# Turned attention rows in a scores bank, one norm per unit, and a memory head prepared ahead

## The chip, the core and the metric

The kernel runs on one core of a Trainium2 chip. The core's engines run side by side, each through its own list of instructions in order: TensorE (PE; its weight loads are PEld), VectorE (DVE), ScalarE (ACT), GpSimd (POOL) and SyncE (SP), which here only starts DMAs. PE writes into PSUM, eight banks of 2 KB a partition; only DVE and ACT read them in this kernel. The metric is the device time of one launch in microseconds (us). About 0.2% (6 us) is what a measurement of this kernel can tell from no change.

## What is computed

One sequence of 512 positions, 1024 channels, passes a hybrid layer and then two further layers, all in float32. Cut to what matters here:

```
x = x + 0.5 * swiglu(norm(x))                     # ffn f1, likewise f2, f3, f4
h = norm(x) @ w_in                                # q, keys and values, gates, conv, memory queries
nsa:  for each of 16 heads: compressed branch + selected branch + window branch,
      each softmax(q.k/8 + rel_bias, masked) @ v, weighted by gates
      (8 blocks of 64 with top 16: all blocks are selected, so both long branches are causal attention)
mem:  4 heads of 256: softmax(qm.km/16) @ vm over 256 memory rows
x = x + (g_nsa*nsa + g_conv*conv + g_mem*mem) @ w_out
second block: stick-breaking attention, ffn, gate; forgetting attention (16 heads, causal), ffn, gate
```

## The kernel before

Every float32 product is made of three matmuls: each operand is split into a rounded high part and a rest (`split`: ACT writes the high part, DVE subtracts), and `mm3` adds high.high, high.low and low.high. A dense step is one `mm3`, three matmuls of 512 columns; a job of eight steps is one 1024x128 weight tile. Its weights come by DMA as `raw` and are split into `wh` (ACT) and `wl` (DVE), three buffers of each.

PSUM is four tags of two banks: `d` for dense results, `s` for scores, `t` for transposes, `o` for attention output. A tag's two banks are used in turn: the third use of a tag waits until the first's readers are done.

`nsa` (from line 934) has 32 units, (head, branch) pairs. In step u of its loop (lines 1046 to 1085) PE makes the scores of unit u (`unit_scores`: three uses of `s`, two dense steps before the last), DVE adds the bias and takes the row minimum (L632), ACT takes the exponential and its row sum (L634), DVE inverts the sum (`RECIPROCAL`) and multiplies it by the gate, POOL scales the four row tiles `pr` (L910). Then the rows of unit u-1 are turned (`unit_turn`): ten 128x128 transposes in three groups, of four, four and two, each group in a bank of `t`, split into `pth` (ACT) and `ptl` (DVE). The third group therefore comes to the first group's bank. `nsa_out` multiplies the turned rows with the values (eight matmuls into `o`). `feed` and `pace` put dense steps of other work (convolution, gates, values) between these; `pinned` keeps PE's matmuls in the order written. DVE, ACT and POOL, and PE where nothing is pinned, are ordered by a scheduler.

`forget` (from line 1301) runs 16 units in the same way; its dense steps are the projections of the later heads and half of the output projection. `head_stats` and `head_norm` normalise queries and keys through banks of `o` and `s`; `normed` in nsa does one head pair, `norm` in forget two, one `s` bank each.

`memory` (from line 683) does four heads one after the other: norm and split of queries, keys and values, scores, softmax, transposes, a gate's dense job and the product. `transpose_rows` (from line 614) turns a row vector such as `rB` into a column `rT`, with one bank of `t` and one copy for each of its four transposes.

Of the kernel before, what the change touches and what calls it, by code (L numbers as in the profile page):

```python
# [12 lines left out]
AF = mybir.ActivationFunctionType  # L13
ALU = mybir.AluOpType
# [149 lines left out]
class Net:  # L164
# [449 lines left out]
    def transpose_rows(self, dst, src, n=S):  # L614

        nc = self.nc
        for i in range(n // P):
            ps = self.bank("t")
            nc.tensor.transpose(ps[:, :P], src[:, i * P : (i + 1) * P], self.ident)
            nc.vector.tensor_copy(dst[:, i : i + 1], ps[:, :1])  # L620


    def softmax_rows(self, pool, src, n, bias, st, i, tag, bufs):
# [59 lines left out]
    def memory(self):  # L683

        nc, tc = self.nc, self.tc
        with self.pool("mem", "left") as pool:
            self.tags = self.TAGS
            qm = []
            for n in range(KC):
                ps = self.dbank()  # L690
                self.dense(ps, self.a["w_qm"][n], self.h)
                q = self.t(pool, S, "qm", 8)
                nc.vector.tensor_tensor(q, ps, self.rB, op=ALU.mult)
                qm.append(q)
            qst = self.head_stats(qm, self.sel256, 2)
            self.tags = ("d",)
            for m in range(4):
                qr, kr = [], []
                for n in (2 * m, 2 * m + 1):
                    self.head_norm(qm[n], n, 2, qst, self.col("mqg")[:, n % 2 : n % 2 + 1])  # L700
                    hl = self.pair(pool, f"qr{n % 2}")
                    self.split(hl[0], hl[1], qm[n], -1.0 / 16.0)
                    qr.append(hl)
                    k = self.t(pool, NM, "kmr", 2)
                    nc.sync.dma_start(k, self.kmd[n * P : (n + 1) * P, :])
                    hl = self.pair(pool, f"kr{n % 2}", NM)
                    self.split(hl[0], hl[1], k)
                    kr.append(hl)
                vr = self.t(pool, S, "vmr", 2)
                nc.sync.dma_start(vr.rearrange("p (i c) -> p i c", i=2),  # L710
                                  self.vmd[:, :, m * 256 : m * 256 + 256].rearrange("i p c -> p i c"))
                vm = self.pair(pool, "vm", S)
                self.split(vm[0], vm[1], vr)
                st = self.t(pool, 2 * NT, "mst", 2)
# [8 lines left out]
                pt = []  # L723
                for i in range(NT):
                    nc.vector.tensor_scalar(pr[i], pr[i], st[:, i : i + 1], None, op0=ALU.mult)
                for b in range(2):
                    tp = self.bank("t")
                    for i in range(NT):
                        nc.tensor.transpose(tp[:, i * P : (i + 1) * P], pr[i][:, b * P : (b + 1) * P], self.ident)
                    hl = self.pair(pool, f"mt{b}")  # L730
                    self.split(hl[0], hl[1], tp)
                    pt.append(hl)
                for n in (2 * m, 2 * m + 1):
                    g = self.t(pool, S, "mg", 2)
                    pg = self.dbank()
                    self.dense(pg, self.a["w_mg"][2, n], self.h)
                    nc.vector.tensor_tensor(g, pg, self.rB, op=ALU.mult)
                    nc.scalar.activation(g, g, AF.Tanh, scale=0.5)
                    po = self.bank("o")
# [172 lines left out]
    def unit_turn(self, pool, pr):  # L912

        ph, pl = self.pair(pool, "pt", 1280, 1)
        for tiles, c0, n in (((0,), 0, 512), ((1, 3), 512, 512), ((2,), 1024, 256)):
            tp = self.bank("t")
            self.feed(2 * (tiles == (2,)))
            for j in tiles:
                for i in range(j, NT):
                    d = self.PT0[j] - c0 + (i - j) * P  # L920
# [13 lines left out]
    def nsa(self):  # L934
        nc, tc = self.nc, self.tc
        self.hv = 1
        with self.pool("nsa", "right") as pool:
# [108 lines left out]
            for u in range(33):  # L1046
# [3 lines left out]
                if u < 32:  # L1050
# [4 lines left out]
                    if br == 1 and u < 31:  # L1055
                        n = u + 1
                        tb = self.nsa_bias(pool, 4 * (2 * (n // 16) + n // 2 % 2) + n // 4 % 4)
                if u == 14:
                    next(cmp0)
                if rows:  # L1060
                    pt = self.unit_turn(pool, rows[0])
                    self.pace(upto - 2)
                    self.nsa_out(pool, V, pc, pt, *rows[1:])
                rows = (pr, a, r, b, br)
                if u == 9:
                    qst = self.head_stats(raw[1], self.sel64, 1, tag="o", fill=1)
                elif u == 10:
                    normed(1, 0, qst)
                    normed(1, 1, qst)
                elif u in (11, 12):  # L1070
                    normed(1, u - 9, qst)
                elif u == 13:
                    cmp0 = self.nsa_cmp(pool, 1, 0, [qn[1, k] for k in range(4)], kc, G, pc)
                    next(cmp0)
                elif u == 14:
# [3 lines left out]
                    kn[0] = keys(1, 0)  # L1079
                elif u == 15:  # L1080
                    next(cmp1)
                    kn[1] = keys(1, 1)
                elif u == 16:
                    next(cmp1, None)
                self.pace(upto)
            self.feed(999)
            self.pinned = False

# [212 lines left out]
    def forget(self):  # L1301
# [3 lines left out]
        with self.pool("fox", "left") as pool:  # L1305
# [73 lines left out]
            for u in range(17):  # L1379
                t, b = u // 2, u % 2  # L1380
                upto = base + (176 - base) * (u + 1) / 10 if u < 10 else 176 + 46 * (u - 9) / 7
                if u < 16:
# [2 lines left out]
                    self.unit_scale(pr, st)  # L1385
                    if u < 15:
                        fb = self.forget_bias(pool, u + 1)
                if rows:
                    pt = self.unit_turn(pool, rows[0])
                    self.pace(upto - 4)  # L1390
                    self.forget_out(pool, m + later, V, pt, *rows[1:])
                rows = (pr, t, b)
                if u % 4 == 1 and u < 13:
                    self.pace(48 * (u // 4 + 1) + 32)
                    hst = self.head_stats(xs[u // 4 + 1], self.sel64, 1, pool=pool, tag="o", fill=2)
                elif u % 4 in (2, 3) and u < 12:
                    n = 2 * (u // 4) + u % 4
                    kq[n] = norm(n, hst)
                self.pace(upto)
            self.feed(999)  # L1400
            self.pinned = False
            self.tags = self.TAGS
# [66 lines left out]
```

## Time and profile before

| what | us |
|---|---|
| median of 3 runs (2928.08 to 2933.24) | 2930.53 |
| the profiled execution | 2931.12 |
| its span, first to last instruction | 2929.3 |
| PE busy | 2858.3 (98%) |
| DVE busy | 1615.2 (55%) |
| ACT busy | 1212.9 (41%) |
| POOL busy | 238.7 (8%) |

The execution was 1.8 us longer than its span. A matmul counts as busy until its pipelined end, so the table's 98% hides short gaps; the views of waits and windows show them. The stages in the trace: memory about 438 to 565 us, the start of nsa to 714, its loop to 1066, the loop of forget 2275 to 2492. The rest is dense layers and the stick-breaking attention, which the change does not touch.

### The profile page before, as it was taken

To read this page: it belongs to the slowest core of one execution; us is meant where nothing else is said; L and a number is where in the kernel's file an instruction comes from. 1 tells how busy PE (TensorE), PEld (TensorE's weight loads), DVE (VectorE), ACT (ScalarE), POOL (GpSimd) and SP (SyncE) were. 2 spreads that over 40 slices of the span, in tenths; PEclk is the share of its full clock that TensorE was granted. 3 is DMA by queue.
4 is the path that set the end of the run, shared out by engine and by line. 5 is a ranking of instruction groups with operands and counts; after the bars stand their busy time and mean duration, and the time that the engine had idled before them with its cause. 6 is when DMAs were issued, how large, how long until landed. Compare 5 with 4: busy or idle time off the path is not lost.

```text
span 2929.3 us, 37143 instructions
## 1 busy us (share of the span) xinstructions
PE 2858.3 (98%) x13873; PEld 2367.6 (81%) x13874; DVE 1615.2 (55%) x2718; ACT 1212.9 (41%) x2078; POOL 238.7 (8%) x361
## 2 busy tenths in 40 slices
PE   9999999999989999999999999999999999999999
PEld 8888887778767888888888887888888777888887
DVE  7443345767666665443347877434357767544344
ACT  6322234344555544322235655223234555422223
POOL 0000000001223320000000000000003431000000
PEclk9999999999999999999999999999999999999999
DMA  7423342235233245323343335232333535522332
GB/s 240 111 94 101 103 131 90 90 119 148 74 98 93 90 142 180 101 94 99 106 130 109 97 104 199 94 101 92 99 99 130 155 101 154 182 100 94 96 93 99
DMA packets 133229, 339.19 MB, mean 116 GB/s; under 512 B 17415, under 2 KB 30215, under 8 KB 133048
## 3 DMA queue, kind: packets, MB, share of 16 engines
q1 hardware_dynamic: 132376, 335.49, 37.0%
q10 hardware_dynamic: 672, 1.32, 0.4%
q8 instruction: 109, 1.79, 0.2%
q14 instruction: 72, 0.59, 0.1%
HBM read 279.82 MB, written 28.61 MB: 105 GB/s over the span
## 4 chain that ended last, share of the span: by engine, by line
PE 63%; DVE 4%; issue 2%; DMA 1%; ACT 1%; POOL 0%; SPq 0%; DVEq 0%; ACTq 0%; POOLq 0%
PE d L190 22%; PE s L190 13%; PE o L190 13%; PE t L190 11%; PE t L195 1%; DMA qk<-xd 1%; DVE wl L219 1%; DVE pr L632 1%; DVE ptl L219 1%; DMA xd<-qk 1%; PE s L1288 0%; PE t L1288 0%; PE o L1298 0%; POOL mo L1172 0%; PE o L1299 0%
## 5 line engine op out<-in xcount | busy, mean ns | idle before, releaser
L209 ACT ACTIVATE wh<-raw 128x1024 fp32r<-128x1024 f32 (+3 forms) x499 | 493.5, 989 | 1205.9 <-PE d L190 339.9
L219 DVE TENSOR_TENSOR wl<-raw,wh 128x1024 fp32r<-128x1024 f32 (+3 forms) x499 | 576.7, 1156 | 302.7 <-ACT wh L209 299.8
L634 ACT ACTIVATE pr<-pr,st 128x128 f32<-128x128 f32 x192 | 106.1, 553 | 68.8 <-DVE st L632 67.9
L910 POOL TENSOR_SCALAR pr<-pr,st 128x128 f32<-128x128 f32 x192 | 106.2, 572 | 244.5 <-DVE st L1384 72.2
L195 PE MATMUL t<-idn,pr 128*128 128x128 f32 x480 | 70.5, 277 | 24.5 <-DVE ptl L219 21.7
L219 DVE TENSOR_TENSOR ptl<-t,pth 128x512 fp32r<-128x512 f32 x144 | 83.3, 595 | 19.4 <-ACT pth L209 18.5
L231 POOL TENSOR_TENSOR raw<-raw,cols 128x1024 f32<-128x1024 f32 x25 | 49.0, 1960 | 523.9 <-DMA xd<-x 466.9
L195 PEld LDWEIGHTS t<-idn,pr 128*128 128x128 f32 x480 | 54.9, 141 | 43.0 <-DVE ptl L219 33.6
L209 ACT ACTIVATE pth<-t 128x512 fp32r<-128x512 f32 x144 | 72.5, 521 | 36.0 <-PE t L195 34.8
L632 DVE CUSTOM_DVE_ANT_0 pr<-s,tb 128x128 f32<-128x128 f32 (+3 forms) x128 | 57.8, 486 | 33.9 <-PE s L190 15.8
L190 PE MATMUL o<-ptl,V 128*128 128x512 f32 x192 | 61.5, 331 | 3.3 <-DVE ptl L219 2.0
L483 ACT ACTIVATE on<-o 64x512 f32<-64x512 f32 x48 | 28.6, 595 | 74.8 <-PE o L190 60.4
L484 DVE TENSOR_TENSOR on<-o,on 64x512 f32<-64x512 f32 x48 | 32.7, 681 | 46.7 <-ACT on L483 46.5
L408 POOL MEMSET hrh<- 128x512 f32 (+2 forms) x10 | 4.7, 471 | 639.2 <-PE s L190 567.1
L190 PE MATMUL o<-pth,V 128*128 128x512 f32 x192 | 56.7, 321 | 0.0
L518 ACT ACTIVATE ta<-ta 128x512 f32<-128x512 f32 x88 | 55.3, 629 | 3.0 <-DVE ta L517 3.0
L190 PE MATMUL d<-h3h,wh 128*128 128x512 f32 x136 | 55.8, 411 | 0.0
L190 PE MATMUL d<-h2h,wh 128*128 128x512 f32 x136 | 55.8, 410 | 0.0
L190 PE MATMUL d<-h0h,wh 128*128 128x512 f32 x136 | 55.1, 405 | 0.4 <-DVE q2s L794 0.4
L190 PE MATMUL d<-h4h,wh 128*128 128x512 f32 x136 | 55.3, 407 | 0.0
L190 PE MATMUL d<-h0h,wl 128*128 128x512 f32 x136 | 53.5, 393 | 1.7 <-DVE wl L219 1.7
L519 DVE TENSOR_TENSOR ta<-s,ta 128x512 f32<-128x512 f32 x22 | 15.2, 692 | 71.2 <-PE s L190 71.2
(2175 smaller groups left out, 8652.8 us busy)
## 6 DMA issues: line engine op xcount, KB each, us to landing
raw<-in_f_in_dram SPq DMA_DIRECT2D x176, 512.0 KB
raw<-in_f_out_dram SPq DMA_DIRECT2D x64, 512.0 KB
raw<-in_f_out_dram SPq DMA_DIRECT2D x32, 384.0 KB
raw<-in_w_mg_dram SPq DMA_DIRECT2D x24, 512.0 KB
raw<-in_w_cv_dram SPq DMA_DIRECT2D x24, 512.0 KB
xd<-x SPq DMA_DIRECT2D x32, 256.0 KB
x<-xd SPq DMA_DIRECT2D x32, 256.0 KB
raw<-in_w_pg_dram SPq DMA_DIRECT2D x16, 512.0 KB
```

The source lines that it names most:

```text
L190: i = self.nc.tensor.matmul(out, lhs, rhs, **kw)
L195: i = self.nc.tensor.transpose(out, src, self.ident)
L209: nc.scalar.activation(h, src, AF.Copy, scale=1.0 if scale is None else scale)
L219: eng.tensor_tensor(lo, src, hb, op=ALU.subtract)
L231: nc.gpsimd.tensor_tensor(v, v, gain.unsqueeze(2).to_broadcast([P, gain.shape[1], n]), op=ALU.mult)
L483: self.nc.scalar.activation(dst[h], po[64:], AF.Copy)
L484: self.nc.vector.tensor_tensor(dst[h], po[:64], dst[h], op=ALU.add)
L518: nc.scalar.activation(ta, ta, AF.Silu)
L519: nc.vector.tensor_tensor(ta, pb, ta, op=ALU.mult)
L632: nc.vector.tensor_tensor_reduce(out=p, in0=src, in1=bias, op0=ALU.add, op1=ALU.min, scale=1.0, scalar=3e38, accum_out=m)
L634: nc.scalar.activation(p, p, AF.Exp, bias=m, scale=-1.0, accum_out=stat)
L910: self.nc.gpsimd.tensor_scalar(pr[i], pr[i], st[:, i : i + 1], 1.0, op0=ALU.mult, op1=ALU.mult)
```

## The change

The third group of a unit's turn goes to a bank of `s`, and no dense steps stand inside the turn. Three steps stand before it and one behind it; the rest of the unit's steps, at least two, come before the product, which is now the last thing in the unit. In nsa `normed` does one head a step (four steps, 10 to 13, where it was two in the first), and the compressed branch of the second half follows a step later. In memory the next head's operands and gates are issued between the softmax scaling and the transposes of the present one. `transpose_rows` writes its four transposes into one bank and copies once.

```diff
     def transpose_rows(self, dst, src, n=S):
+        ps = self.bank("t")
         for i in range(n // P):
-            ps = self.bank("t")
-            nc.tensor.transpose(ps[:, :P], src[:, i * P : (i + 1) * P], self.ident)
-            nc.vector.tensor_copy(dst[:, i : i + 1], ps[:, :1])
+            self.tr(ps[:, i * P : (i + 1) * P], src[:, i * P : (i + 1) * P])
+        nc.vector.tensor_copy(dst, ps.rearrange("p (i c) -> p i c", c=P)[:, : n // P, 0])
...  memory
+            def gates(m):     # the two dense jobs w_mg[2, n] of head m with their tanh, "mg" now 4 buffers
+            def operands(m):  # norm, split and loads of head m as before, "vm" now 2 buffers
+            gs = gates(0)
+            nxt = operands(0)
             for m in range(4):
+                qr, kr, vm = nxt
...
                     nc.vector.tensor_scalar(pr[i], pr[i], st[:, i : i + 1], None, op0=ALU.mult)
+                now = gs
+                if m < 3:
+                    nxt = operands(m + 1)
+                    gs = gates(m + 1)
...  unit_turn
         for tiles, c0, n in (((0,), 0, 512), ((1, 3), 512, 512), ((2,), 1024, 256)):
-            tp = self.bank("t")
-            self.feed(2 * (tiles == (2,)))
+            tp = self.bank("s" if tiles == (2,) else "t")
...  nsa, the loop over u
-                if u == 14:
-                    next(cmp0)
+                self.feed(3)
                 if rows:
                     pt = self.unit_turn(pool, rows[0])
-                    self.pace(upto - 2)
-                    self.nsa_out(pool, V, pc, pt, *rows[1:])
-                rows = (pr, a, r, b, br)
+                    self.feed(1)
...
-                elif u == 10:
-                    normed(1, 0, qst)
-                    normed(1, 1, qst)
-                elif u in (11, 12):
-                    normed(1, u - 9, qst)
-                elif u == 13:
+                elif 10 <= u <= 13:
+                    normed(1, u - 10, qst)
+                elif u == 14:
                     cmp0 = self.nsa_cmp(pool, 1, 0, [qn[1, k] for k in range(4)], kc, G, pc)
...
-                self.pace(upto)
+                self.pace(max(upto, self.steps + 2))
+                if rows:
+                    self.nsa_out(pool, V, pc, pt, *rows[1:])
+                rows = (pr, a, r, b, br)
...  forget, the loop over u
+                self.feed(4)
                 if rows:
                     pt = self.unit_turn(pool, rows[0])
-                    self.pace(upto - 4)
-                    self.forget_out(pool, m + later, V, pt, *rows[1:])
-                rows = (pr, t, b)
+                    self.feed(1)
...  head_stats and norm as before
-                self.pace(upto)
+                self.pace(max(upto, self.steps + 2))
+                if rows:
+                    self.forget_out(pool, m + later, V, pt, *rows[1:])
+                rows = (pr, t, b)
```

How the order moves, at three places. A row is an instruction of that engine, line, operation, what it writes and reads; `x2` merges equal ones.

PE in the loop of nsa, turn of the first unit, from the end of the second group, before:

```order
L195 MATMUL t_5966<-idn_148,pr_1088_5858 128x128 x2
L190 MATMUL d_5980<-h0h_77,wh_5773 128x512
L190 MATMUL d_5980<-h0l_78,wh_5773 128x512
L190 MATMUL d_5980<-h0h_77,wl_5774 128x512
L190 MATMUL d_5980<-h1h_79,wh_5773 128x512
L190 MATMUL d_5980<-h1l_80,wh_5773 128x512
L190 MATMUL d_5980<-h1h_79,wl_5774 128x512
L195 MATMUL t_5973<-idn_148,pr_1086_5838 128x128
L195 MATMUL t_5973<-idn_148,pr_1088_5858 128x128
L190 MATMUL d_5980<-h2h_81,wh_5773 128x512
```

and now:

```order
L195 MATMUL t_5974<-idn_148,pr_1084_5850 128x128 x2
L195 MATMUL s_5981<-idn_148,pr_1082_5830 128x128
L195 MATMUL s_5981<-idn_148,pr_1084_5850 128x128
L190 MATMUL d_5955<-h3h_83,wh_5765 128x512
L190 MATMUL d_5955<-h3l_84,wh_5765 128x512
L190 MATMUL d_5955<-h3h_83,wl_5766 128x512
L190 MATMUL d_5955<-h4h_85,wh_5765 128x512
L190 MATMUL d_5955<-h4l_86,wh_5765 128x512
L190 MATMUL d_5955<-h4h_85,wl_5766 128x512
L190 MATMUL d_5955<-h5h_87,wh_5765 128x512
L190 MATMUL d_5955<-h5l_88,wh_5765 128x512
```

The two transposes of the third group wrote `t_5973` behind six dense matmuls; they now write `s_5981` right behind the second group, and nine dense matmuls follow. Nine more now stand ahead of the turn.

DVE in a late unit of nsa, from the last score tile, before (`pr,st<-s,tb` is the softmax step of L632, `ptl<-t` the split of a turned group, `st<-st,G` the gate):

```order
L632 ISA pr_1728_9107,st_9080<-s_9104,tb_9014 128x512
L632 ISA st_9080 128x1
L219 TENSOR_TENSOR ptl_9117<-t_9118,pth_9116 128x512
L1052 RECIPROCAL st_9080<-st_9080 128x4
L1053 TENSOR_TENSOR st_9080<-st_9080,G_4487 128x4
L219 TENSOR_TENSOR ptl_9117<-t_9125,pth_9116 128x512
L219 TENSOR_TENSOR ptl_9117<-t_9132,pth_9116 128x256
L484 TENSOR_TENSOR on_9157<-o_9053,on_9157 64x512
```

and now:

```order
L632 ISA pr_1724_9105,st_9078<-s_9102,tb_9012 128x512
L632 ISA st_9078 128x1
L1068 RECIPROCAL st_9078<-st_9078 128x4
L1069 TENSOR_TENSOR st_9078<-st_9078,G_4479 128x4
L775 TENSOR_TENSOR cv_9027<-d_9057,cv_9027 128x512
L219 TENSOR_TENSOR wl_9334<-raw_9331,wh_9333 128x1024
L219 TENSOR_TENSOR ptl_9130<-t_9131,pth_9129 128x512
L779 SCALAR_TENSOR_TENSOR cv_9124<-cv_9027,cols_71,cv_9124 128x511
L219 TENSOR_TENSOR ptl_9130<-t_9138,pth_9129 128x512
L780 SCALAR_TENSOR_TENSOR cv_9124<-cv_9027,cols_71,cv_9124 128x510
L219 TENSOR_TENSOR ptl_9130<-s_9145,pth_9129 128x256
```

The three splits stood around the reciprocal; now the reciprocal and the gate, the convolution's multiplications (`cv`) and a weight split (`wl`) stand ahead of the splits and among them.

PE in forget, the norm of the next heads (`s<-hrh` and `s<-hrl`: two matmuls into one bank), before, behind the product:

```order
L190 MATMUL o_19402<-ptl_19370,V_18773 128x256
L190 MATMUL o_19402<-pth_19369,V_18773 128x256
L190 MATMUL s_19415<-hrh_19313,selr_151 128x512
L190 MATMUL s_19415<-hrl_19314,selr_151 128x512
L190 MATMUL s_19419<-hrh_19313,selr_151 128x512
L190 MATMUL s_19419<-hrl_19314,selr_151 128x512
L190 MATMUL d_19348<-wh_19092,h6h_89 128x256
```

and now, behind the turn:

```order
L195 MATMUL s_19402<-idn_148,pr_3484_19107 128x128
L195 MATMUL s_19402<-idn_148,pr_3486_19120 128x128
L190 MATMUL d_19376<-h3h_83,wh_19141 128x512
L190 MATMUL d_19376<-h3l_84,wh_19141 128x512
L190 MATMUL d_19376<-h3h_83,wl_19142 128x512
L190 MATMUL s_19410<-hrh_19281,selr_151 128x512
L190 MATMUL s_19410<-hrl_19282,selr_151 128x512
L190 MATMUL s_19414<-hrh_19281,selr_151 128x512
L190 MATMUL s_19414<-hrl_19282,selr_151 128x512
L190 MATMUL d_19376<-h4h_85,wh_19141 128x512
```

The norm moved from behind the product to three matmuls behind the third group. `s_19402` (third group), `s_19410` and `s_19414` are three uses of the tag `s` in a row.

## Rows read from the trace of the kernel before

**Rows 1.** The page, part 4: the chain that ended last, shares of the span

```profile
PE 63%; DVE 4%; issue 2%; DMA 1%; ACT 1%; POOL 0%; SPq 0%; DVEq 0%; ACTq 0%; POOLq 0%
```

**Rows 2.** Windows: length, busy us of PE, PEld, DVE, ACT, POOL; clock, DMA

```profile
438.00:565.00 127.00, 122.68 (x584) 97.16 (x583) 76.34 (x131) 57.73 (x105) 6.25 (x14) 1.00 0.28 94
...
714.00:1066.00 352.00, 326.26 (x1726) 271.58 (x1725) 224.86 (x551) 185.66 (x438) 100.58 (x150) 0.99 0.31 88
2283.00:2492.00 209.00, 198.82 (x1161) 163.22 (x1161) 152.03 (x324) 123.03 (x279) 62.81 (x80) 0.99 0.46 133
843.00:846.50 3.50, 3.50 (x10) 2.87 (x11) 0.92 (x2) 0.38 (x1) 1.52 (x3) 0.55 0.67 127
```

**Rows 3.** PE waits, 714:1066 (first loop): who for whom: us, times, longest

```profile
PE t L195 <- DVE ptl L219: 17.7, 18, 3.5
PE s L190 <- DVE st L632: 2.9, 3, 1.0
PE t L195 <- DVE st L1053: 2.5, 1, 2.5
PE o L190 <- DVE nrr L219: 1.9, 1, 1.9
```

**Rows 4.** PE timeline, one unit: start, us, what [idle before <-releaser]

```profile
744.72 1.03 PE L195 MATMUL t<-idn,pr 128*128 128x128 f32 x8
...
748.52 0.44 PE L195 MATMUL t<-idn,pr 128*128 128x128 f32 x2 [1.37 <-DVE ptl L219]
748.72 0.48 PE L190 MATMUL d<-h2h,wh 128*128 128x512 f32 x1
749.03 0.40 PE L190 MATMUL d<-h2l,wh 128*128 128x512 f32 x1
```

**Rows 5.** DVE timeline, the same unit

```profile
744.53 0.69 DVE L758 TENSOR_TENSOR cv<-d,cv 128x512 f32<-128x512 f32 x1 [0.58 <-PE d L190]
745.14 0.68 DVE L632 CUSTOM_DVE_ANT_0 pr<-s,tb 128x512 f32<-128x512 f32 x1
...
745.75 1.22 DVE L219 TENSOR_TENSOR wl<-raw,wh 128x1024 fp32r<-128x1024 f32 x1
746.88 0.75 DVE L762 SCALAR_TENSOR_TENSOR cv<-cv,cols,cv 128x511 f32<-128x511 f32 x1
...
747.77 0.69 DVE L219 TENSOR_TENSOR ptl<-t,pth 128x512 fp32r<-128x512 f32 x1
...
749.11 1.02 DVE L219 TENSOR_TENSOR ptl<-t,pth 128x512 fp32r<-128x512 f32 x2
```

**Rows 6.** ACT timeline, the same unit

```profile
744.67 1.04 ACT L209 ACTIVATE wh<-raw 128x1024 fp32r<-128x1024 f32 x1
...
746.32 0.71 ACT L634 ACTIVATE pr<-pr,st 128x512 f32<-128x512 f32 x1
```

**Rows 7.** DVE and then POOL timeline, a later unit

```profile
1001.01 2.28 DVE L219 TENSOR_TENSOR wl<-raw,wh 128x1024 fp32r<-128x1024 f32 x1 [0.18 <-ACT wh L209]
...
1000.91 1.29 POOL L754 TENSOR_TENSOR cv<-cv,rB 128x512 f32<-128x512 f32 x1 [1.44 <-DVE cv L753]
```

**Rows 8.** PE waits, 2275:2492 (second loop)

```profile
PE t L195 <- DVE ptl L219: 4.1, 5, 2.1
PE o L190 <- DVE ptl L219: 2.0, 4, 0.6
PE s L190 <- DVE x L423: 1.7, 4, 0.6
```

**Rows 9.** PE timeline, the four transposes of rB at the start of nsa

```profile
587.76 0.69 PE L619 MATMUL t<-idn,rB 128*128 128x128 f32 x2 [4.12 <-DVE rT L620]
...
589.10 0.63 PE L190 MATMUL d<-h2h,wh 128*128 128x512 f32 x1
589.52 0.63 PE L190 MATMUL d<-h2l,wh 128*128 128x512 f32 x1
```

**Rows 10.** PE waits, 438:565 (memory)

```profile
PE s L190 <- ACT mp L630: 2.9, 3, 1.5
```

More of the change, by code (lines that the diff above doesn't have):

```diff
@@ L696, in memory @@
             self.tags = ("d",)
-            for m in range(4):
+            def gates(m):
+                gs = []
+                for n in (2 * m, 2 * m + 1):
+                    g = self.t(pool, S, "mg", 4)
+                    pg = self.dbank()
+                    self.dense(pg, self.a["w_mg"][2, n], self.h)
+                    nc.vector.tensor_tensor(g, pg, self.rB, op=ALU.mult)
+                    nc.scalar.activation(g, g, AF.Tanh, scale=0.5)
+                    gs.append(g)
+                return gs
+            def operands(m):
                 qr, kr = [], []
@@ L711, in memory @@
                                   self.vmd[:, :, m * 256 : m * 256 + 256].rearrange("i p c -> p i c"))
-                vm = self.pair(pool, "vm", S)
+                vm = self.pair(pool, "vm", S, 2)
                 self.split(vm[0], vm[1], vr)
+                return qr, kr, vm
+            gs = gates(0)
+            nxt = operands(0)
+            for m in range(4):
+                qr, kr, vm = nxt
                 st = self.t(pool, 2 * NT, "mst", 2)
@@ L722, in memory @@
                 nc.vector.reciprocal(st[:, :NT], st[:, :NT])
-                pt = []
                 for i in range(NT):
                     nc.vector.tensor_scalar(pr[i], pr[i], st[:, i : i + 1], None, op0=ALU.mult)
+                now = gs
+                if m < 3:
+                    nxt = operands(m + 1)
+                    gs = gates(m + 1)
+                pt = []
                 for b in range(2):
@@ L728, in memory @@
                     for i in range(NT):
-                        nc.tensor.transpose(tp[:, i * P : (i + 1) * P], pr[i][:, b * P : (b + 1) * P], self.ident)
+                        self.tr(tp[:, i * P : (i + 1) * P], pr[i][:, b * P : (b + 1) * P])
                     hl = self.pair(pool, f"mt{b}")
@@ L733, in memory @@
                 for n in (2 * m, 2 * m + 1):
[L734 to L739, printed above, removed]
+                    g, po = now[n % 2], self.bank("o")
                     for b in range(2):
@@ L1057, in nsa @@
                         tb = self.nsa_bias(pool, 4 * (2 * (n // 16) + n // 2 % 2) + n // 4 % 4)
-                if u == 14:
-                    next(cmp0)
+                self.feed(3)
                 if rows:
                     pt = self.unit_turn(pool, rows[0])
-                    self.pace(upto - 2)
-                    self.nsa_out(pool, V, pc, pt, *rows[1:])
-                rows = (pr, a, r, b, br)
+                    self.feed(1)
                 if u == 9:
                     qst = self.head_stats(raw[1], self.sel64, 1, tag="o", fill=1)
-                elif u == 10:
-                    normed(1, 0, qst)
-                    normed(1, 1, qst)
-                elif u in (11, 12):
-                    normed(1, u - 9, qst)
-                elif u == 13:
+                elif 10 <= u <= 13:
+                    normed(1, u - 10, qst)
+                elif u == 14:
                     cmp0 = self.nsa_cmp(pool, 1, 0, [qn[1, k] for k in range(4)], kc, G, pc)
                     next(cmp0)
-                elif u == 14:
+                    kn[0] = keys(1, 0)
+                elif u == 15:
+                    next(cmp0)
+                    kn[1] = keys(1, 1)
+                elif u == 16:
                     next(cmp0, None)
@@ L1078, in nsa @@
                     next(cmp1)
[L1079 to L1083, printed above, removed]
+                elif 17 <= u <= 18:
                     next(cmp1, None)
-                self.pace(upto)
+                self.pace(max(upto, self.steps + 2))
+                if rows:
+                    self.nsa_out(pool, V, pc, pt, *rows[1:])
+                rows = (pr, a, r, b, br)
             self.feed(999)
```

## The prediction

> **What bounds the kernel now.** I read the chain of waits first: PE holds 63% of it, the next engine 4% [rows 1]. Then the windows of the stages that the change touches. In the loop of nsa PE is busy 326.26 of 352.00 us, DVE 224.86, ACT 185.66 and POOL 100.58 [rows 2]: PE is the bound and the other engines have slack on the mean. Both kernels give PE the same matmuls here, so the change can move only three things: PE's idle time, the clock it is granted, and what it pays where matmuls of two kinds meet. The idle time is 352.00 - 326.26 = 25.7 us in nsa's loop, 209.00 - 198.82 = 10.2 in forget's and 127.00 - 122.68 = 4.3 in memory [rows 2]. The lists of waits say who caused it: 17.7 us of nsa's are transposes that wait for the split `ptl` [rows 3], 4.1 us of forget's [rows 8], and one transpose of `rB` waits 4.12 us for a copy of one column [rows 9].
>
> One unit shows the mechanism. PE ends eight transposes and six dense matmuls, and the third group then idles 1.37 us [rows 4], because it needs the first group's bank, whose split DVE starts at 747.77. DVE is late since it did a weight split of 1.22 us and a convolution step of 0.75 us first [rows 5].
>
> **nsa, what goes.** The third group takes a bank of `s`, free since the softmax step of the unit's second score tile. So the 17.7 us go. The 2.5 us of the one first group that waits for the gate go too, since nine more matmuls stand ahead of the turn, and the 1.9 us of `o`, which is asked for later [rows 3]. That is 22.1. The mean granted clock of the loop is 0.99; 0.01 of 352 us is 3.5 us, with rounding 1.8 to 5.3. One stretch of it, of 3.5 us, has 0.55 [rows 2], so it lost about 3.5 x 0.45 = 1.6. I take two such stretches as gone: 3.0. The first dense matmul behind transposes takes 0.48 us against 0.40 for the next [rows 4]; there is one such meeting less a unit, 32 x 0.08 = 2.6. Together 27.7 us.
>
> **nsa, what is late next.** The splits are not done earlier, only the product is asked for later, so it may now wait for `ptl`. A dense matmul follows the next after 0.42 us in a stretch at half clock [rows 9], so after 0.21 at full. In a late unit I count from PE's last score matmul. PE has nine dense matmuls (1.9 us), ten transposes (eight take 1.03 [rows 4], so 1.3) and nine dense ones (1.9), and asks for the product at 5.1. DVE takes the row minimum (0.68 [rows 5]), ACT the exponential (0.71 [rows 6]); with the handings over that is 1.8. Reciprocal and gate, two tiny instructions, bring it to 2.2; the convolution's multiplication (0.69) to 2.9; the weight split (1.22) to 4.2; the first `ptl` (0.69) to 4.9, a convolution step (0.75) to 5.6, the second `ptl` to 6.3 [rows 5]. The product consumes the first group's high parts first, so it waits about 1 us where both convolution steps stand among the splits, half that where one stands, nothing in the other two kinds of unit. Over the thirteen late units that is a mean of 0.4.
>
> The weight split took 2.28 us instead of 1.22 where it ran beside a multiplication on POOL [rows 7, 5]. It now stands just behind the gate, which is when POOL begins to scale the rows. The bounds of this are nothing and 1.06 a unit; I take 0.15, since the other splits near POOL's work in the unit above kept 0.69 [rows 5]. So 13 x 0.55 = 7 us.
>
> The Trainium skill, page "SBUF — State Buffer", section "Who interferes with whom", says that a DVE instruction with two inputs in SBUF and a GpSimd instruction that reads SBUF shut each other out. By that rule the weight split, which has two such inputs, would pay up to the whole 1.06 us in each late unit, and the time would be that of the first rival. The trace agrees in the one place shown, 2.28 against 1.22 us [rows 7, 5].
>
> The ten units in the middle also carry a norm or the compressed branch: one or two more instructions of about 0.7 us on DVE [rows 5] ahead of the splits. Here I take 0.95 each, 9.5 us, between 0 and the 1.37 of the unit shown [rows 4]. The early units have few other DVE steps: 1 us. Given back: 17.5. Net of nsa's loop: 10.2 us less.
>
> **forget.** What goes: 4.1 + 2.0 + 1.7 us of waits [rows 8], 16 x 0.08 = 1.3 of meetings, and about 1.6 of slow clock (0.99 of 209 us gives 1.0 to 3.1 [rows 2]): 10.7. What comes: in six units two norms follow the turn by three matmuls. With the third group they are three uses of `s`, so the second norm waits until the third group's split, DVE's last of the three, is done. PE reaches it about 0.6 + 2 x 0.21 us behind the group, DVE needs two or three instructions of 0.69 [rows 5] from there: some 1.2 us each, 7.2. And in the last three units the dense steps run out (two to five matmuls between turn and product instead of nine), so that the product waits about 1.2 us each, 3.6. Net about nothing; bounds 8 less and 17 more.
>
> **rB's transposes.** Four transposes through two banks with four copies become four in one bank with one copy. The 4.12 us go. Behind them matmuls follow at 0.42 us instead of 0.21 [rows 9]; I take a dozen, 2.4 us. The weight split behind them may now be late by half of its 1.22 us [rows 5]: 0.6 back. Net 5.9 less. The other calls of the function stand where I saw no such wait, and are costed at nothing.
>
> **Memory.** The next head's operands and gates now lie under the softmax of the present one. PE idles 4.3 us in the stage [rows 2], of which 2.9 for the softmax's rows [rows 10]. DVE is busy 76.34 of 127.00 us [rows 2], but the head's norms come in bunches, and moved ahead they can hold up the same softmax. Bounds: 4.3 less, 2 more; I take half of the idle time, 2.2 less. The change issues the gates' and values' weight loads one head earlier on SP; DMA is busy 0.28 of this stage [rows 2], so I cost that at nothing; were a load late, PE would show a wait on a weight split of a microsecond or two, inside the bound.
>
> **Sum.** -10.2 + 0.1 - 5.9 - 2.2 = -18.2. The profiled execution took 2931.12, so 2912.9; the median shown is 0.6 lower: 2912.3, say 2912.
>
> **Rivals.** First: the waits merely move from the bank to the product. Weight split and convolution stand ahead of the splits, and POOL's scaling beside them stretches them by the whole 1.06 us: 0.9 more in each of thirteen late units (12) and 0.3 in the ten others (3). For it: the 2.28 us [rows 7]. Against it: DVE is busy 224.86 of 352 us [rows 2], so a late split is caught up within the unit. Time: 2912 + 15 = 2927.
>
> Second, the other side: the ring of `s`. It now serves three score tiles, a turn group and, in forget, two norms, so a late `ptl` holds back norms and next scores instead of one turn. It decides once the second norm waits over 2 us, for then the clock falls as behind the 4.12 us [rows 9]: 2.5 + 1.2 each, six norms 22, and the three last units 2 each, 6; less the 10.7 that go, forget is 17.5 worse. If nsa then gives all of its 27.7 back through the same ring, rB and memory alone remain, 8.1 less: +9.4, so 2940. For it: DVE is busy 152.03 of 209 us in forget [rows 2], the fullest of the loops. Against it: no wait on a `ptl` there was over 2.1 us [rows 8].
>
> Third: the dense steps cover all. Nine matmuls and the transposes are 5.1 us, close to what DVE needs; where the scheduler's order fits, the product waits only in the units with the most steps. nsa 22 less, forget 8, rB 6.5, memory 4.3: -40.8, so 2890. For it: even the old cover of six matmuls left only 18 waits in 32 units [rows 3].
>
> **How the numbers follow.** Forecast 0.54, its own range 2900 to 2923 (the product's wait in nsa from 0.2 to 0.9 a unit). First rival 0.18, second 0.10, third 0.18. The range for 8 in 10 is 2892 to 2930: it takes in the first rival, and leaves out half of the third and the second. A measurement can tell 0.2%, 6 us, from no change. Forecast, third rival and a fourth of the first are faster by more: 0.77. The rest of the first is no change: 0.13. The second is slower: 0.10.
>
> **What the profile after would show.** No transpose waiting for `ptl` in either loop, and no 4.12 us at `rB`; instead `PE o <- DVE ptl` in nsa's loop, about 17 us in all, and in forget `PE s <- DVE ptl` before the second norm, about six times 1.2. PE's busy time in the windows stays near 326 and 199 us. Wrong would be: `o <- ptl` of 25 us or more in nsa (first rival) or under 6 (third); norms in forget that wait over 2 us with a granted clock near 0.55 behind them (second); a wait for a weight split in memory.

## The result, and the profile after

The changed kernel took 2911.93 us (median of 4 runs, 2910.13 to 2913.31) against 2931.7 for the kernel before: ratio 0.9934, 95% interval 0.9917 to 0.9951, so 14 to 24 us less. Forecast were 2912 and a range of 2892 to 2930. The total is met almost to the microsecond, and so it says little; the parts have to be held against the trace one by one.

The profiled execution took 2910.92 us. Windows of memory, of nsa's loop and of forget's loop, in the columns of [rows 2]; the stages are shorter, so the windows are:

```profile
438.00:561.00 123.00, 122.42 (x587) 97.89 (x586) 76.98 (x129) 58.05 (x105) 6.41 (x14) 1.00 0.30 97
702.00:1042.00 340.00, 323.92 (x1724) 271.66 (x1723) 225.82 (x549) 185.84 (x437) 119.04 (x150) 0.99 0.33 91
2261.00:2474.00 213.00, 202.47 (x1185) 167.55 (x1184) 153.14 (x326) 123.61 (x282) 67.87 (x80) 0.99 0.47 133
```

Memory lost its idle time: 4.3 us in [rows 2], 0.6 now. nsa's loop is 12 us shorter at nearly the same busy time of PE, so it is idle time that went (25.7, now 16.1). Forget's loop kept its idle time: 10.2, now 10.5. POOL is busy 119.04 us in nsa's loop, 100.58 before, with the same 150 instructions; more of that below.

Who makes PE wait in nsa's loop, first list, and in forget's, second, against [rows 3] and [rows 8]:

```profile
PE o L190 <- DVE ptl L219: 5.0, 11, 0.8
PE t L195 <- DVE ptl L219: 3.8, 3, 1.7
PE t L195 <- issue: 2.6, 1, 2.6
PE s L190 <- DVE st L632: 2.1, 2, 1.8
PE o L190 <- DVE nrr L219: 1.9, 1, 1.9
...
PE s L190 <- DVE ptl L219: 6.1, 6, 2.1
```

The 17.7 us of the third group are gone, but the 3.8 us of `t <- ptl` are new and in another place: units 15 to 18, where the compressed branch's four transposes follow the turn by three matmuls. PE's timeline there:

```profile
871.59 1.03 PE L195 MATMUL t<-idn,pr 128*128 128x128 f32 x8
...
872.60 0.48 PE L190 MATMUL d<-h0h,wh 128*128 128x512 f32 x1
...
875.23 0.63 PE L195 MATMUL t<-idn,cp 128*128 128x128 f32 x4 [1.69 <-DVE ptl L219]
```

The eight transposes take both banks of `t`, so `cp` is the third use, as the third group was before. The 2.6 us of `issue` are the same branch at another point: its scores' sum on DVE, `cp<-s,cp`, stands behind the three splits and ends at 892.91, and the transposes that read it start at 893.01. The 6.1 us in forget are the second norm, at the place that the prediction named, up to 2.1 us long, and behind that one the granted clock is 0.50 from 2353.97 to 2357 us (0.42 us from one dense matmul to the next, about 0.23 elsewhere):

```profile
2353.97 0.79 PE L190 MATMUL s<-hrh,selr 128*128 128x512 f32 x1 [2.06 <-DVE ptl L219]
...
2354.99 0.63 PE L190 MATMUL d<-h1h,wh 128*128 128x512 f32 x1
2355.41 0.63 PE L190 MATMUL d<-h1l,wh 128*128 128x512 f32 x1
```

A late unit of nsa shows the product's wait. First PE, then DVE:

```profile
1020.47 0.40 PE L190 MATMUL s<-k0l,q2s 128*128 128x512 f32 x1
...
1023.62 0.38 PE L195 MATMUL s<-idn,pr 128*128 128x128 f32 x2
...
1025.92 0.40 PE L190 MATMUL o<-ptl,V 128*128 128x512 f32 x1
...
1027.38 0.44 PE L190 MATMUL o<-ptl,V 128*128 128x384 f32 x1 [0.83 <-DVE ptl L219]
...
1028.37 0.39 PE L190 MATMUL o<-ptl,V 128*128 128x256 f32 x1 [0.21 <-DVE ptl L219]
```

```profile
1021.01 0.69 DVE L632 CUSTOM_DVE_ANT_0 pr<-s,tb 128x512 f32<-128x512 f32 x1 [1.09 <-PE s L190]
...
1023.02 0.69 DVE L775 TENSOR_TENSOR cv<-d,cv 128x512 f32<-128x512 f32 x1
1023.81 1.25 DVE L219 TENSOR_TENSOR wl<-raw,wh 128x1024 fp32r<-128x1024 f32 x1
1024.98 0.68 DVE L219 TENSOR_TENSOR ptl<-t,pth 128x512 fp32r<-128x512 f32 x1
1025.59 1.14 DVE L779 SCALAR_TENSOR_TENSOR cv<-cv,cols,cv 128x511 f32<-128x511 f32 x1
1026.64 0.68 DVE L219 TENSOR_TENSOR ptl<-t,pth 128x512 fp32r<-128x512 f32 x1
...
1027.90 0.41 DVE L219 TENSOR_TENSOR ptl<-s,pth 128x256 fp32r<-128x256 f32 x1
```

From the last score matmul to the first product matmul are 5.4 us (forecast 5.1), to the end of the second split 6.8 (forecast 6.3), and the waits add to 1.04 (forecast 1). The chain was right for this kind of unit. Note what stands ahead of the first split: a convolution step and a weight split.

### The profile page after: what moved, and what is told of

Its sections match the earlier page's. It is cut to its first block, busy times and chain, and to the rows that moved or that the text cites. A ratio compares the mean times of both kernels' runs of the same rounds, so it can differ in the third digit from the quotient of the medians.

```text
span 2909.1 us, 37129 instructions
## 1 busy us (share of the span) xinstructions
PE 2852.0 (98%) x13873; PEld 2365.5 (81%) x13874; DVE 1615.8 (56%) x2708; ACT 1212.1 (42%) x2078; POOL 263.5 (9%) x361
## 4 chain that ended last, share of the span: by engine, by line
PE 87%; DVE 6%; issue 2%; DMA 2%; ACT 2%; POOL 0%; SPq 0%; DVEq 0%; POOLq 0%; ACTq 0%
PE d L190 31%; PE s L190 19%; PE o L190 18%; PE t L190 15%; DVE wl L219 2%; PE t L195 1%; ACT wh L209 1%; DVE ptl L219 1%; DMA qk<-xd 1%; PE s L1301 0%; PE t L1301 0%; PE o L1311 0%; DVE cv L833 0%; PE o L1312 0%; POOL mo L1185 0%
## 5 line engine op out<-in xcount | busy, mean ns | idle before, releaser
L927 POOL TENSOR_SCALAR pr<-pr,st 128x128 f32<-128x128 f32 x192 | 132.5, 708 | 301.0 <-PE t L195 181.4
L632 DVE CUSTOM_DVE_ANT_0 pr<-s,tb 128x128 f32<-128x128 f32 (+3 forms) x128 | 58.9, 487 | 67.5 <-PE s L190 50.7
L219 DVE TENSOR_TENSOR ptl<-t,pth 128x512 fp32r<-128x512 f32 x96 | 62.3, 681 | 15.0 <-ACT pth L209 14.8
L209 ACT ACTIVATE pth<-t 128x512 fp32r<-128x512 f32 x96 | 53.0, 592 | 15.6 <-PE t L195 14.9
L519 DVE TENSOR_TENSOR ta<-t,ta 128x512 f32<-128x512 f32 x22 | 15.2, 691 | 70.9 <-PE t L190 70.8
L190 PE MATMUL d<-h1h,wh 128*128 128x512 f32 x136 | 54.2, 399 | 0.0
L190 PE MATMUL d<-h3l,wh 128*128 128x512 f32 x136 | 53.8, 396 | 0.0
```

The source lines that it names most:

```text
L190: i = self.nc.tensor.matmul(out, lhs, rhs, **kw)
L209: nc.scalar.activation(h, src, AF.Copy, scale=1.0 if scale is None else scale)
L219: eng.tensor_tensor(lo, src, hb, op=ALU.subtract)
L519: nc.vector.tensor_tensor(ta, pb, ta, op=ALU.mult)
L632: nc.vector.tensor_tensor_reduce(out=p, in0=src, in1=bias, op0=ALU.add, op1=ALU.min, scale=1.0, scalar=3e38, accum_out=m)
L927: self.nc.gpsimd.tensor_scalar(pr[i], pr[i], st[:, i : i + 1], 1.0, op0=ALU.mult, op1=ALU.mult)
```

## The experiments

Below, a stretch is the difference of the start times of two matmuls in a profile. nsa's runs from its loop's first product matmul that reads `pth` to the stick-breaking stage's first matmul that reads `sp3h`; forget's from the first matmul of its first norm (`s<-hrh`) to the first matmul `o<-pt0h` of the last gate, so that a projection and a feed-forward layer are in it; memory's from its first score to the first transpose of `rB`; `rB`'s from there to the first product of the compressed values.

| kernel | us | ratio to before (95%) | memory | rB | nsa | forget |
|---|---|---|---|---|---|---|
| before | 2930.5 to 2932.4 | 1 | 80.7 | 14.8 | 825.8 | 604.3 |
| changed | 2911.93 | 0.9934 (0.9917 to 0.9951) | 75.5 | 7.4 | 813.6 | 605.7 |
| transpose_rows alone | 2925.43 | 0.9973 (0.9962 to 0.9985) | 80.7 | 7.5 | 825.2 | 601.6 |
| memory alone | 2927.54 | 0.9983 (0.9972 to 0.9993) | 75.5 | 14.7 | 825.5 | 602.6 |
| bank alone | 2907.27 | 0.9913 (0.9892 to 0.9935) | 80.7 | 13.9 | 807.9 | 598.6 |
| changed, third group in `t` | 2999.78 | 1.0228 (1.0200 to 1.0257) | 75.6 | 7.5 | 886.3 | 624.5 |
| changed, branch in `s` | 2913.14 | 0.9938 (0.9923 to 0.9954) | 75.5 | 7.4 | 812.3 | 606.0 |
| changed, norm behind product | 2915.55 | 0.9946 (0.9929 to 0.9963) | 75.7 | 7.5 | 815.3 | 608.8 |
| changed, two norms in a step | 2916.34 | 0.9948 (0.9934 to 0.9963) | 75.5 | 7.5 | 817.6 | 607.4 |
| three gains | 2894.59 | 0.9879 (0.9864 to 0.9894) | 75.6 | 7.4 | 809.2 | 597.8 |
| three gains, steps ahead | 2932.43 | 0.9997 (0.9988 to 1.0007) | 75.6 | 7.4 | 824.6 | 616.8 |
| changed, no steps ahead | 2897.50 | 0.9883 (0.9860 to 0.9905) | 75.5 | 7.5 | 807.8 | 597.0 |
| three gains, new schedule | 2889.45 | 0.9859 (0.9839 to 0.9878) | 75.5 | 7.5 | 804.3 | 599.1 |

Forget's loop is the same in the first, third and fourth rows, and its stretch is 601.6 to 604.3: below 3 us such a difference is not read. nsa's three agree within 0.6. Between nsa's stretch and forget's lie stages that no edit touches; they took 716.2 to 720.9 us.

**transpose_rows alone.**

```diff
+        ps = self.bank("t")
         for i in range(n // P):
-            ps = self.bank("t")
-            nc.tensor.transpose(ps[:, :P], src[:, i * P : (i + 1) * P], self.ident)
-            nc.vector.tensor_copy(dst[:, i : i + 1], ps[:, :1])
+            self.tr(ps[:, i * P : (i + 1) * P], src[:, i * P : (i + 1) * P])
+        nc.vector.tensor_copy(dst, ps.rearrange("p (i c) -> p i c", c=P)[:, : n // P, 0])
```

> The kernel before with the new transpose_rows alone (one bank, one copy). Theory: the 4.12 us wait at the first call and the slow clock behind it go, 7.4 us by the landmarks of the two profiles (the stretch from the first transpose of rB to the first product of the compressed values, 14.8 us before, 7.4 after); the other two calls give nothing: 2923 to 2924. Rival: the wait only moves to the weight split that follows, so that at most 3 us go: 2927 to 2930.

The theory holds: 7.3 us of the stretch, and the rival's 3 us are excluded by it. The total fell by 7.9 (4.4 to 11.1). In the changed kernel the place of [rows 9] reads:

```profile
576.10 0.60 PE L195 MATMUL t<-idn,rB 128*128 128x128 f32 x4
...
578.39 0.50 PE L190 MATMUL d<-h0h,wl 128*128 128x512 f32 x1 [0.60 <-DVE wl L219]
```

No wait over 0.6 us, and the granted clock is 1.00 from 577 to 582 us.

**Memory alone.** Edit: `gates(m)` and `operands(m)` as the change has them, issued between the scaling and the transposes of head m-1.

> The kernel before with the new memory attention alone (the next head's operands and gates issued ahead). Theory: the stretch from the head's norms to the first transpose of rB is 4.4 us shorter (142.5 before, 137.8 after, of which 0.3 lies before it): 2926 to 2927. Rival: a part of that comes from the new transpose_rows behind it, since DVE reaches the copies earlier; then memory alone gives under 2 us: 2929 to 2930.

The stretch is 5.2 us shorter and `rB`'s is not, so the rival falls. The gains of memory and transpose_rows are separate and add.

**The bank alone, and the bank taken back.** In the kernel before (its dense steps and product untouched):

```diff
         for tiles, c0, n in (((0,), 0, 512), ((1, 3), 512, 512), ((2,), 1024, 256)):
-            tp = self.bank("t")
+            tp = self.bank("s" if tiles == (2,) else "t")
             self.feed(2 * (tiles == (2,)))
```

> The kernel before with the third group of a turn in a bank of the scores and nothing else: the two dense steps inside the turn and the order of the product stay. Theory one (the bank is the wait, the steps behind the turn cover the splits): the 17.7 us of transposes waiting for ptl go from nsa's loop, but only two dense steps stand between the turn and the product, so some 9 to 12 us come back as a product that waits for ptl; nsa's loop 5 to 9 us shorter, forget 1 to 3, total 2919 to 2925. Rival (the dense steps on both sides do the work, the bank by itself only moves the wait): nsa's loop 0 to 3 us shorter, total 2927 to 2931.

In the changed kernel the same expression becomes `self.bank("t")`, with the steps where the change put them:

> The changed kernel with the third group back in a bank of t, its dense steps on both sides as changed. Theory one (the bank is the wait): the third group stands right behind the second and waits for the first group's split in every unit, 1 to 3 us each in 32 units of nsa and 16 of forget; 50 to 140 us longer, 2960 to 3050. Rival (the nine matmuls ahead of the turn are cover enough, since DVE has reached the split by then): under 0.5 us a unit, 2915 to 2935.

The bank is the wait: back in `t`, the third group waits in every unit of nsa, and nsa's stretch grows by 73 us:

```profile
PE t L195 <- DVE ptl L219: 56.0, 32, 2.8
```

But neither theory foresaw the first of the two. The bank alone gives 17.9 us in nsa and 3 to 6 in forget, more than all four edits together, and hardly anything comes back. PE's waits in nsa's loop, then in forget's:

```profile
PE o L190 <- DVE ptl L219: 3.1, 5, 1.4
...
PE t L195 <- DVE st L1053: 2.5, 1, 2.5
...
PE o L190 <- DVE ptl L219: 2.8, 6, 0.8
```

So the other edits of the loops, together, cost 5.7 us in nsa and about 7 in forget. Which of them?

**Three suspects, one at a time.** First the compressed branch, its transposes moved to the ring of `s` (`tp = self.bank("s")`, `tq = self.bank("s")` for the second half's two calls):

> The changed kernel with the compressed branch of nsa's second half turned in banks of s instead of t. Theory one (in units 15 to 18 the compressed branch's four transposes are the third use of t, three matmuls behind the turn, and have taken over the wait of the old third group): the three waits for ptl of 1.2 to 1.9 us go with the slow clock behind them; the 2.7 us of the fourth stay, since they are for POOL's product; nsa's loop 5 to 7 us shorter, 2905 to 2907. Rival (that time is DVE's work in these units, so it comes back as a product or a score that waits): under 2 us, 2910 to 2912.

The rival was nearer. The three waits on `t` went and 1.3 us of nsa's stretch came of it, since a wait of 2.1 us on `s` and more waiting products (5.6 us for 5.0) took their place; the 2.6 us of `issue` stayed:

```profile
PE s L190 <- DVE ptl L219: 2.1, 1, 2.1
```

Then forget's norm, behind the product again:

```diff
-                elif u % 4 in (2, 3) and u < 12:
-                    n = 2 * (u // 4) + u % 4
-                    kq[n] = norm(n, hst)
                 self.pace(max(upto, self.steps + 2))
                 if rows:
                     self.forget_out(pool, m + later, V, pt, *rows[1:])
+                if u % 4 in (2, 3) and u < 12:
+                    n = 2 * (u // 4) + u % 4
+                    kq[n] = norm(n, hst)
```

> The changed kernel with forget's norm of the next heads back behind the product. Theory one (the second norm waits for the third group's split because the group took its bank): the 6.1 us of norms waiting for ptl go, and some slow clock; as in the kernel before, about 2 us of scores that wait for the norm's x come back; forget 4 to 6 us shorter, 2906 to 2908. Rival (what forget lost is the dense steps that run out in its last units): under 2 us, 2910 to 2912.

The theory fell: forget is not shorter (608.8 against 605.7). The 6.1 us went, but the next scores now follow the norm with no dense step between and wait for it instead, twelve times, and others for the row minima:

```profile
PE s L190 <- DVE x L423: 4.9, 12, 0.6
PE s L190 <- DVE st L632: 4.9, 8, 1.2
```

Then nsa's norms:

```diff
-                elif 10 <= u <= 13:
-                    normed(1, u - 10, qst)
+                elif u == 10:
+                    normed(1, 0, qst)
+                    normed(1, 1, qst)
+                elif u in (11, 12):
+                    normed(1, u - 9, qst)
```

> The changed kernel with the first two of nsa's four norms in one step again (10, 10, 11, 12 for 10 to 13); the compressed branch stays where it was changed to. Theory one (a norm is a bank of s; two in one step wait for the third group's split as in forget): one wait of 1 to 2 us with a slow clock more, 2912 to 2915. Rival (one norm a step is no help, and frees no wait): 2911 to 2912, no norm waiting in the list.

One new line, and the stretch is 4 us longer; the wait is longer than expected:

```profile
PE s L190 <- DVE ptl L219: 3.2, 1, 3.2
```

So one norm a step is a gain inside this change, not its cost. No suspect by itself was the cause: moving a wait's victim only finds the next one, which points to the splits being late for all of them.

**Three gains together.** The kernel before with the bank, transpose_rows and memory, and none of the moves.

> The kernel before with the bank, the new transpose_rows and the new memory attention, and none of the moves of dense steps, product, norm and compressed branch. Theory one (the moves cost what the bank alone had beyond the changed kernel, 5.7 us in nsa and 7.1 in forget): the gains add, 24 for the bank, 7 and 4.5, against 2931 to 2932: 2895 to 2898, faster than the changed kernel by 13 to 17. Rival (part of the gain of the bank alone was the clock or a shift that another start of nsa takes away): 2900 to 2908.

They add, and it beats the changed kernel by 17 us. What is left to explain is then the moves alone, in both directions.

**The steps ahead of the turn.** To the three gains, steps ahead are added (the product stays); and from the changed kernel, they are taken away (the product stays last, and the steps come between turn and product):

```diff
+                self.feed(3)   # nsa; in forget self.feed(4)
                 if rows:
                     pt = self.unit_turn(pool, rows[0])
                     self.pace(upto - 2)
...
-                self.feed(3)   # nsa; in forget self.feed(4)
                 if rows:
                     pt = self.unit_turn(pool, rows[0])
                     self.feed(1)
```

> The kernel of the three gains (bank, transpose_rows, memory) with one move of the change added: three dense steps ahead of the turn in nsa, four in forget; the two steps inside the turn and the product stay in place. Theory two (the steps ahead of the turn cost: they make the turn later, and the order of DVE then has a convolution step and a weight split ahead of the splits, where the splits came first): the product waits for ptl 1 to 2 us in half of the units, nsa's stretch to the stick-breaking stage 820 to 835 us against 808 to 809, forget's 600 to 610 against 598; total 2907 to 2925. Rival (the product as the last thing costs, the steps ahead do not): both stretches within 2 us, 2893 to 2900.

> The changed kernel without the dense steps ahead of the turn (three in nsa, four in forget), which then come between the turn and the product. Theory two (the steps ahead of the turn cost): the splits come first on DVE again and the product, asked for later still, waits for ptl under 3 us in nsa; the compressed branch's third use of t and forget's second norm still wait, 4 to 7 and 3 to 6 us; nsa's stretch 806 to 811, forget's 600 to 604, total 2897 to 2905. Rival (the late product and the norm ahead of it cost): as the changed kernel, nsa 812 to 815, forget 604 to 608, 2909 to 2915.

This settles that the steps ahead cost, in both loops: 15.4 us in nsa and 19.0 in forget where the product stands in its old place, and 5.8 and 8.7 where it is last. In forget that is more than theory two had (616.8 for 600 to 610), and so is the total (2932.43 for 2907 to 2925). The late product is no cost in forget, which with no steps ahead takes 597.0 with it and 597.8 without. In nsa no product waits with it, but scores wait 8.4 us for a row minimum; the last kernel below differs from this one in the places of the product and of the dense steps around it alone, has 3.1 us of that wait, and a stretch 3.5 us shorter. The largest wait with the steps added, nsa:

```profile
PE o L190 <- DVE ptl L219: 13.6, 9, 2.0
```

and with the steps taken away, nsa and then forget:

```profile
PE s L190 <- DVE st L632: 8.4, 7, 2.5
PE t L195 <- DVE ptl L219: 2.6, 3, 2.2
...
PE s L190 <- DVE x L423: 4.2, 5, 0.9
...
PE s L190 <- DVE ptl L219: 1.2, 1, 1.2
```

DVE of the latter kernel, in the same unit as the one shown above, tells why its product no longer waits:

```profile
1014.25 0.69 DVE L632 CUSTOM_DVE_ANT_0 pr<-s,tb 128x512 f32<-128x512 f32 x1 [1.01 <-PE t L195]
...
1015.27 0.69 DVE L219 TENSOR_TENSOR ptl<-t,pth 128x512 fp32r<-128x512 f32 x1 [0.32 <-ACT pth L209]
...
1016.46 0.69 DVE L219 TENSOR_TENSOR ptl<-t,pth 128x512 fp32r<-128x512 f32 x1
1017.07 0.41 DVE L219 TENSOR_TENSOR ptl<-s,pth 128x256 fp32r<-128x256 f32 x1
1018.75 0.69 DVE L775 TENSOR_TENSOR cv<-d,cv 128x512 f32<-128x512 f32 x1 [1.27 <-PE d L190]
1019.55 1.23 DVE L219 TENSOR_TENSOR wl<-raw,wh 128x1024 fp32r<-128x1024 f32 x1
```

The splits follow the row minimum at once and end 3.2 us after it began; the convolution and the weight split come behind. In the changed kernel they stand ahead and among, and the last split ends 7.3 us after the row minimum began (1021.01 to 1028.31). The nine matmuls ahead end a dense job, and its evacuation and the next weight split are then due on DVE before the turn is. They are no cover for the product, which stands behind the turn: between third group and product PE has nine dense matmuls in this unit of the changed kernel, and eighteen without the steps ahead.

But the steps ahead do not cost alike in every unit. With the three gains they leave no dense matmul between third group and product, where there were six, and still the first 24 steps of the loop take 2.0 us less than without them, counted from score to score. The whole cost arises in the last eight steps. There a dense job ends inside every turn (in the turns before, inside two), and from 965 to 1052 us 10.6 us of products wait, at a granted clock of 0.92; without the steps ahead that window has no waiting product and a clock of 1.00. DVE and then PE there:

```profile
1034.73 0.69 DVE L775 TENSOR_TENSOR cv<-d,cv 128x512 f32<-128x512 f32 x1
1035.51 1.23 DVE L219 TENSOR_TENSOR wl<-raw,wh 128x1024 fp32r<-128x1024 f32 x1
...
1037.32 0.42 DVE L219 TENSOR_TENSOR ptl<-s,pth 128x256 fp32r<-128x256 f32 x1
...
1037.79 0.39 PE L190 MATMUL o<-ptl,V 128*128 128x256 f32 x1 [1.96 <-DVE ptl L219]
```

So what costs there is a job that ends ahead of a split, with no cover behind the turn, and not each step ahead. Nor does the late unit account for the 5.8 us of the changed kernel. Its late units have 3.6 us of waiting products, and without the steps ahead 2.9 us of waiting scores in their place, so that 1 to 2 us are won there. Nearly half of the 5.8 (a dense matmul that moved counted at 0.23 us) is there by the end of step 9, where the statistics wait 1.9 us for their own split (`nrr`), 0.2 without the steps ahead; the rest arises in the units between. In forget PE's waits are 10.5 us with the late product and the steps ahead and 8.0 without these, for 8.7 us of stretch. The steps ahead also use up its dense steps early (the loop's last step has 3 dense matmuls, 33 without). What either is worth there was not tested.

**The new schedule on the three gains.** One norm a step, the branch behind the turn and a step later, nothing else:

> The kernel of the three gains with nsa's new schedule of norms and compressed branch (one norm a step, the branch behind the turn and a step later); dense steps and product as before. Theory: the first group's wait for the gate (2.5 us and the slow clock behind it) goes, and the branch's transposes, with dense steps and the product ahead of them, do not wait for a bank of t: nsa 2 to 5 us shorter than with the three gains, 2890 to 2893. Rival (the branch behind the turn is the third use of t as in the changed kernel): 3 to 7 us of waits come, 2896 to 2902.

The theory holds: 4.9 us less in nsa, and the best of all versions, 22 us under the changed kernel. The wait for the gate is gone and no new line has taken its place:

```profile
PE s L190 <- DVE st L632: 3.1, 4, 1.0
PE o L190 <- DVE ptl L219: 2.1, 4, 1.1
```

## Why the prediction came out right, point by point

- **The bound.** Right: PE's work stayed and idle time went.
- **rB's transposes.** Right in kind, a little small: 5.9 forecast, 7.3 measured. The 0.6 us that the weight split was to give back are no term: PE waits 0.6 us for it, but it waited 0.9 at the same matmul before.
- **Memory.** Right in kind, mis-sized: I took half of the idle time, 2.2 us; 5.2 went, slightly over the bound of 4.3. All three waits for the softmax's rows went, and the norms that I feared would hold up the softmax did not.
- **nsa, what goes.** The 17.7 us went, and the bank alone does it. The 1.9 us of `o` did not go: they are a wait of the statistics on their own split (`nrr`), 1.9 us in the changed kernel too; I had read the line as one of the product. The wait for the gate goes by either of two ways: it is gone with the new schedule of the branch alone, and 0.4 us of it are left with the old schedule and the matmuls ahead of the turn.
- **nsa, what comes.** The sum of 17.5 us was near (13.5 of the 16.1 us of idle time now stand in the four lines above other than `nrr`, and the longest have slow clock behind them), and its parts were not. The late units are right in kind and half the size (7 forecast; 3.6 measured, with 1.04 us where both convolution steps stand among the splits, as forecast, and no weight split stretched). The ten middle units were given 9.5 us of waiting products; products wait 5.0 us in the whole loop, and the middle units wait at the compressed branch's third use of `t` (3.8), for the branch's sum of scores on DVE (2.6) and at the scores behind it (2.1). The prediction spoke of the ring of `s` alone and overlooked that of `t`. One slip stands in it besides: the product takes each group's low part first, not the high.
- **forget.** Forecast at nothing, measured 1.4 us longer in the pair of profiles and about 3 over all, which is no more than the stretch varies. The second norm's wait is there, 6.1 us for 7.2; the products of the last units were to wait 3.6 us, and in the whole loop products wait 1.0.
- **The step that failed** is one that the sum treats as given: that steps on both sides of the turn are cover. I took the order of DVE, weight split and convolution ahead of the splits, as a fact of the units; in the late units it is a consequence of the three steps ahead. Part of what I booked as the price of moving the wait was the price of one edit: without it nsa's stretch is 5.8 us shorter, forget's 8.7, and the time is 2897.5. The error did not show in the total because the order that I read was that of the changed kernel.
- **The total.** That it fits to the microsecond is luck. By the table the four stretches fell by 5.2 + 7.4 + 12.2 - 1.4 = 23.4 us, where the sum had 18.2; the profiled execution fell by 20.2, and 2.6 of the difference are in the untouched stages between nsa and forget (716.2 before, 718.8 now).
- **The rivals.** The first did not come: product waits of 5.0 us, not over 25, and no weight split in a late unit was stretched. The second came in its mechanism, far below its price: 6.1 us over six norms, with a slow clock behind one, where it had 2.5 and 1.2 for each. The third's sign came and its time did not: I had said that product waits under 6 us, where I expected 17, would mean the third, and that no transpose would wait for `ptl`; products wait 5.0, and the compressed branch's transposes wait 3.8. Its 2890 is the time of another kernel, the new schedule on the old order (2889.45), which has no steps ahead, so not by its mechanism.

## What to carry to other kernels

Where a wait is for a bank, change the tag first and time it alone, before steps are moved around it: here that alone was worth more than the whole change. Ask of filler work on the bounding engine what it brings to the engine that is late. Here the steps ahead of the turn cost nothing in 24 steps of nsa's loop, and 15.4 us in the last eight, where a dense job ended there and its evacuation and the next weight split came ahead of a split that PE waited for. A total that agrees with a forecast proves none of its terms; the stretches of the profile and a few one-edit kernels do.

## What the runs showed of the hardware

Where a weight split on DVE and a POOL instruction meet, one of them is stretched, and in the meetings shown here it was the later one. Where POOL's multiplication had begun first, the split was long; the changed kernel, POOL and then DVE:

```profile
721.19 1.30 POOL L771 TENSOR_TENSOR cv<-cv,rB 128x512 f32<-128x512 f32 x1 [4.98 <-DVE cv L770]
```

```profile
721.68 1.90 DVE L219 TENSOR_TENSOR wl<-raw,wh 128x1024 fp32r<-128x1024 f32 x1
```

In the late units the split kept its 1.22 to 1.25 us, and POOL's four scalings around it took longer; an early unit where no weight split ran beside them, and the late unit shown above:

```profile
742.20 2.05 POOL L927 TENSOR_SCALAR pr<-pr,st 128x128 f32<-128x128 f32 x4 [5.09 <-PE t L195]
...
1023.16 3.02 POOL L927 TENSOR_SCALAR pr<-pr,st 128x128 f32<-128x128 f32 x4 [5.34 <-PE t L195]
```

That is where POOL's 18.5 us more in nsa's loop are (119.04 against 100.58), and the list of PE's waits there has no line for them. The Trainium skill, page "SBUF — State Buffer", section "Who interferes with whom", calls the shared port pair an exclusive lock. The trace agrees with that; the prediction took the rule as a price of up to 1.06 us a unit on DVE, and in the late units it was paid on POOL.
